# Ordering the heads' transposes and pooled products behind the second next projection product, with low output weights made by VectorE

## The chip, the core and the metric

The kernel runs on one core of a Trainium2 chip. The metric is the device time of one execution in microseconds (us); a kernel's time is the median of its runs.

## What is computed

One layer of a hybrid encoder, on two sequences (1024 and 2048 tokens of width 1024) that share their weights. `mem` is 256 further tokens for each sequence. Cut to what matters:

```python
h = rms_norm(x, norm_pre)
z = h @ w_in                                   # 1024 -> 2304 columns
u_pool, g_pool, q, k, v, g_attn, q_x, g_x = split(z)
pool_out = multiscale_pool(u_pool, pool_w, pool_scale) * silu(g_pool)   # windows 2, 4, 8, 16: (window mean - u) @ pool_w[g], scaled
q = rope(rms_norm(q per head, q_norm))         # 8 heads of 64
k = rope(rms_norm(k per head, k_norm))         # 2 heads of 64
attn_out = softmax(q k^T / 8) v * silu(g_attn)
k_m, v_m = split(rms_norm(mem, mem_norm) @ w_mem_kv)
x_out = softmax(q_x k_m^T / 8) v_m * silu(g_x)
y = x + rms_norm(concat(pool_out, attn_out, x_out) @ w_out, norm_post)
```

All inputs and outputs are float32.

## The kernel before

The program has two parts. In the first, up to about 700 us, the projections `h @ w_in` are made and their results stored to DRAM scratch; in the second, attention, output projection and final norm read them back. The second part's order is written out by hand and is not touched by the change.

**Stages of the projections.** The tokens are worked in super-blocks of 1024, each of two blocks of 512: first `mem`, then the short sequence ("prompt stage"), then the two halves of the long one ("first" and "second sample stage"). For each block the normalised input is transposed on TensorE (`pt` tiles, line 621) into `hT_hi` and `hT_lo`: each float32 number is kept as a rounded high part and the low rest, and a product is made of three matmuls (high with high, high with low, low with high). The columns of `w_in` are cut into six groups of 384, and a group is run over both blocks before the next. Their order is n1, ct0, n0, ct2, ct1, ct3. While a group runs, the next group's weights are loaded (`wraw`) and split, by ScalarE into `w_hi` (line 649) and by VectorE into `w_lo` (line 652).

- n1 and n0 make *natural* products (tokens on partitions, 384 columns): four tiles of 128 tokens per block. n1 holds two query heads, the two key heads and v; n0 the other six query heads.
- The ct groups make *transposed* products (128 columns on partitions, 512 tokens), three per block. ct0 holds the two pooling chunks (c = 0 and 1) and a gate.

Each product is 8 x 3 matmuls into one PSUM tile `pz` (four buffers), by `product` (lines 660 to 662).

**The heads' chain.** Behind each natural product, `norm_rope` turns the result into normalised, rotated heads: ScalarE copies it to `z` (723) and squares it to `sq` (724); VectorE sums per head (726) and scales (70); GpSimd raises to the power -0.5 (`rs`, 72) and multiplies by the rotary tables (`t1` 734, `sq` 739); VectorE adds and scales `t1` (745, 746; the profile's name for it is `t`). `heads_transposed` then transposes `t1` on TensorE into the PSUM tile `ptq` (758), ScalarE and VectorE split it into high and low (`qst`, 77 and 78), and SP's queue stores it. `z`, `sq`, `t1` and `qst` have two buffers each.

**The pooling chain.** Behind each pooling product, ScalarE copies it to `u` (842), GpSimd makes window sums by adding shifted copies (851, tiles `s2`, `s4`, `sm`, one buffer each), VectorE copies one half (864) and forms mean minus `u` in `sm` (872). TensorE multiplies by `pool_w` into `pm` (879), which shares its two PSUM buffers with `ptq`, and ScalarE scales the result into `s4` (881), from where it is stored.

**Output weights.** In the sample stages, sixteen pieces of `w_out` are split: a load into `woraw` (775), the high part by ScalarE (776), the low part `wost` by GpSimd (777), a store (778).

**What sets the order.** In the projections a scheduler orders each engine's instructions by a model of their durations; every engine then runs its own list strictly in order and waits on semaphores. `behind(e, first)` adds a dependence of instruction `e` on the last instruction in the list `first`. Buffers of a pool are handed out in program order.

Of the kernel before, what the change touches and what calls it, by code (L numbers as in the profile page):

```python
# [7 lines left out]
F32 = mybir.dt.float32  # L8
F32R = mybir.dt.float32r
AF = mybir.ActivationFunctionType  # L10
ALU = mybir.AluOpType
# [12 lines left out]
def encoder(ctx, tc, I, O):  # L24


    nc = tc.nc
# [8 lines left out]
    DQ = {}  # L36
# [9 lines left out]
    DP = [scratch(f"dp{s}", [128, 2, T]) for s, (_, T) in enumerate(SEQS)]  # L46
# [455 lines left out]
    for g in groups:  # L502
        n, c = first[g], g.chunks // 2
        g.early = g in pairs[0].groups
        at(n + (1.2 if g.kind == 1 and g.s == 0 else 0.2), g.load_late)
        k = 0
# [61 lines left out]
    with ExitStack() as p1:  # L568
# [70 lines left out]
        def weights(src, pieces):  # L639
# [13 lines left out]
                                               in1=hi[:, c, 0:n].bitcast(F32), op0=ALU.mult, op1=ALU.subtract)  # L653
            return hi, lo

        def product(ps, terms, beside=lambda: None):

            n = len(terms)
            for c, (sh, sl, mh, ml) in enumerate(terms):
                nc.tensor.matmul(ps, lhsT=sh, rhs=mh, start=c == 0, stop=False)  # L660
                nc.tensor.matmul(ps, lhsT=sh, rhs=ml, start=False, stop=False)  # L661
                nc.tensor.matmul(ps, lhsT=sl, rhs=mh, start=False, stop=c == n - 1)  # L662
                if c % 2:
                    beside()

        def natural(hT, w, i, col, width):

# [48 lines left out]
        def norm_rope(ps, parts, tt):  # L716

            n = sum(h for h, _ in parts)
            w = 64 * n
            z = ftwo.tile([128, 384], F32, name="z", tag="z")  # L720
            sq = ftwo.tile([128, 384], F32, name="sq", tag="sq")
            t1 = ftwo.tile([128, 384], F32, name="t1", tag="t1")
            nc.scalar.copy(out=z[:, 0:w], in_=ps[:, 0:w])
            nc.scalar.activation(out=sq[:, 0:w], in_=ps[:, 0:w], func=AF.Square)  # L724
            ss = ftwo.tile([128, 6], F32, name="ssh", tag="ssh")
            nc.vector.tensor_reduce(out=ss[:, 0:n],
                                    in_=sq[:, 0:w].rearrange("p (h d) -> p h d", d=64),
                                    axis=AX.X, op=ALU.add)
            r = rsqrt(ftwo, ss[:, 0:n], n, 64, f"rsh{n}")
            h0 = 0  # L730
            for heads, (C, S) in parts:
                cols = slice(64 * h0, 64 * (h0 + heads))
                v3 = "p (h d) -> p h d"
                nc.gpsimd.tensor_tensor(
                    out=t1[:, cols].rearrange(v3, d=64), in0=z[:, cols].rearrange(v3, d=64),
                    in1=C[:, tt:tt + 1].broadcast_to([128, heads, 64]), op=ALU.mult)
                v5 = "p (h x s r) -> p h x s r"
                for s in range(2):
                    nc.gpsimd.tensor_tensor(
                        out=sq[:, cols].rearrange(v5, x=2, s=2, r=16)[:, :, :, s],  # L740
                        in0=z[:, cols].rearrange(v5, x=2, s=2, r=16)[:, :, :, 1 - s],
                        in1=S[:, tt:tt + 1].rearrange("p n (x s r) -> p n x s r", x=2, s=2)[:, :, :, s]
                        .broadcast_to([128, heads, 2, 16]), op=ALU.mult)
                h0 += heads
            nc.vector.tensor_tensor(out=t1[:, 0:w], in0=t1[:, 0:w], in1=sq[:, 0:w], op=ALU.add)
            nc.vector.tensor_tensor(
                out=t1[:, 0:w].rearrange("p (h d) -> p h d", d=64),
                in0=t1[:, 0:w].rearrange("p (h d) -> p h d", d=64),
                in1=r.unsqueeze(2).broadcast_to([128, n, 64]), op=ALU.mult)
            return t1  # L750
# [3 lines left out]
        def heads_transposed(src, npair, keys=None):  # L754

            pt = pst.tile([128, 4, 128], F32, name="ptq", tag="ptq")
            for c in range(npair):
                nc.tensor.transpose(out=pt[:, c], in_=src[:, 128 * c:128 * c + 128], identity=ident)
            o = ftwo.tile([128, 2, 3, 128], F32R, name="qst", tag="qst")
            split(o[:, 0, 0:npair], o[:, 1, 0:npair], pt[:, 0:npair])  # L760
            if keys is not None:
                old = steps[keys % 2]
                d = pt[:, 1]
                if keys > 1:
                    d = ftwo.tile([128, 128], F32, name="kstep", tag="kstep")
                    nc.vector.tensor_tensor(out=d, in0=pt[:, 1], in1=old, op=ALU.subtract)
                split(o[:, 0, 2], o[:, 1, 2], d)
                nc.scalar.copy(out=old, in_=pt[:, 1])
            return o
        def split_w_out(n):  # L770

            c, x = n // 2, slice(512 * (n % 2), 512 * (n % 2) + 512)
            raw = ftwo.tile([128, 512], F32, name="woraw", tag="woraw")
            both = ftwo.tile([128, 2, 512], F32R, name="wost", tag="wost")
            behind(nc.sync.dma_start(out=raw, in_=I["w_out"][0, 128 * c:128 * c + 128, x]), gated)
            nc.scalar.copy(out=both[:, 0], in_=raw)
            nc.gpsimd.tensor_tensor(out=both[:, 1], in0=raw, in1=both[:, 0].bitcast(F32), op=ALU.subtract)
            nc.sync.dma_start(out=DWO[c][:, :, x].rearrange("x p f -> p x f"), in_=both.bitcast(F32))


        def store_heads(o, c, dst, j):
            nc.sync.dma_start(out=dst, in_=o[64 * j:64 * j + 64, :, c].bitcast(F32))

        def group_n0(s, b, hT, w):
            for i in range(4):
                tt = 4 * b + i
                ps = natural(hT, w, i, 0, 384)
                o = heads_transposed(norm_rope(ps, [(6, rope["q"])], tt), 3)
                for j in range(2):
                    nc.sync.dma_start(  # L790
                        out=DQ[s, tt // 2, 0][j, :, :, tt % 2],
                        in_=o[64 * j:64 * j + 64, :, 0:2].bitcast(F32))
                    store_heads(o, 2, DQ[s, tt // 2, 1][j, :, :, tt % 2, 0], j)

        def group_n1(s, b, hT, w):
            if not rope:
                rope_tables()
            rope_block(b)
            for i in range(4):
                tt = 4 * b + i  # L800
                ps = natural(hT, w, i, 0, 384)
                vst = ftwo.tile([128, 2, 64], F32, name="vst", tag="vst")
                nc.scalar.copy(out=vst, in_=ps[:, 256:384].rearrange("p (g d) -> p g d", d=64))
                nc.scalar.dma_start(out=DV[s][:, :, tt].rearrange("g p x -> p g x"), in_=vst)
                o = heads_transposed(norm_rope(ps, [(2, rope["q"]), (2, rope["k"])], tt), 2, tt)
                keys = slice(128 * tt, 128 * tt + 128)
                for j in range(2):
                    store_heads(o, 0, DQ[s, tt // 2, 1][j, :, :, tt % 2, 1], j)
                    store_heads(o, 2, DK[s][j][1:3, :, keys].rearrange("x d t -> d x t"), j)
                    nc.sync.dma_start(out=DK[s][j][0, :, keys], in_=o[64 * j:64 * j + 64, 0, 1].bitcast(F32))  # L810

        poolw = one.tile([128, 2, 128], F32, name="poolw")
        pscale = one.tile([128, 2], F32, name="pscale")
# [15 lines left out]
        def pool_chunk(s, b, c, ps):  # L829
# [15 lines left out]
                nc.vector.memset(u[:, 528:L], 0.0)  # L845
            s2 = one.tile([128, L], F32, name="s2", tag="s2")
            s4 = one.tile([128, L], F32, name="s4", tag="s4")
            sm = one.tile([128, L], F32, name="sm", tag="sm")

            def add(out, a, sh, lo, hi, rows_):  # L850
                nc.gpsimd.tensor_tensor(out=out[rows_, lo:hi], in0=a[rows_, lo - sh[0]:hi - sh[0]],
# [17 lines left out]
            if last:  # L869
# [2 lines left out]
            nc.vector.scalar_tensor_tensor(out=sm[:, lo:hi], in0=sm[:, lo:hi],  # L872
                                           scalar=invw[:, c:c + 1], in1=u[:, lo:hi],
                                           op0=ALU.mult, op1=ALU.subtract)
            at = lo
            while at < hi:
                n = min(512, hi - at)
                pm = pst.tile([128, 512], F32, name="pm", tag="ptq")
                nc.tensor.matmul(pm[:, 0:n], lhsT=poolw[:, c], rhs=sm[:, at:at + n],
                                 start=True, stop=True)  # L880
                nc.scalar.activation(out=s4[:, at:at + n], in_=pm[:, 0:n], func=AF.Copy, scale=pscale[:, c:c + 1])
                at += n
            t0 = 512 * b - 16
            nc.scalar.dma_start(out=DP[s][:, c, t0 + lo:t0 + hi], in_=s4[:, lo:hi])

        def gate_chunk(s, b, kind, c, ps):
            g = one.tile([128, 512], F32, name="gst", tag="gst", bufs=2)
# [78 lines left out]
        rope = {}  # L966
# [4 lines left out]
        for sb, (kind, s, nb, b0) in enumerate(SB):  # L971
            groups = groups_of(sb)
            nxt = []
            for gi, (src, pieces, run) in enumerate(groups):
# [5 lines left out]
                final = gi + 1 == len(groups)  # L980
                last = sb + 1 == len(SB)
                if last and gi == 3:
                    front.close()
                    front_open = False
                    early = ctx.enter_context(tc.tile_pool(name="early", bufs=1, side="right", reuse_waits="tile"))
                    open_early()
                    for g in loads.pop(-1):
                        g.load()
# [139 lines left out]
```

## Time and profile before

| | |
|---|---|
| median of 3 runs | 1708.17 us (1707.6 to 1708.54) |
| the profiled execution | 1707.39 us |
| its span, first to last instruction | 1705.6 us |
| TensorE busy | 1674.2 us of the span |
| VectorE, GpSimd, ScalarE busy | 1146.1, 844.2, 826.7 us |
| mean granted TensorE clock | 0.998 |

The profile shows one execution. In its rows PE is TensorE, PEld its weight loads, DVE VectorE, ACT ScalarE, POOL GpSimd and SP the queue that issues most DMAs. A row of a group of instructions gives the line, engine, operation, output<-inputs, the shapes and the count, then busy us and mean ns of one, then how long the engine stood idle just ahead of them and what ended that. A row in order of time begins with the start and the duration in us. A matmul's start is recorded, its end is modelled, and matmuls overlap, so distances from start to start are the safer measure.

### The profile page before, as it was taken

Reading aid. Unit: us, or ns where it says so; the run is one execution under the profiler, and the core shown is the slowest. Engines: PE = TensorE matmul, PEld = TensorE weight load, DVE = VectorE, ACT = ScalarE, POOL = GpSimd, SP = SyncE. Lnnn points to the kernel's source line nnn. Section 1 sums busy time; section 2 is a strip of 40 time slices with the busy share of each in tenths; the row PEclk is TensorE's granted clock in tenths of the full one; section 3 lists DMA queues with packets and bytes.
Section 4 is the critical chain, followed back from the end, with each engine's and each line's share of the span. In section 5 each row is a group of like instructions: output and inputs, shape, how many; then the busy total and the mean of one; then the engine's idle time right before and its main releaser. Section 6 shows DMA issues by size and latency. Waiting matters only on the chain. (4 is left out here: it accounts for less than half of the span.)

```text
span 1705.6 us, 26342 instructions
## 1 busy us (share of the span) xinstructions
PE 1674.2 (98%) x9400; PEld 1166.7 (68%) x9400; DVE 1146.1 (67%) x1791; ACT 826.7 (48%) x1392; POOL 844.2 (49%) x814
## 2 busy tenths in 40 slices
PE   7999999999999999999999999999999999999998
PEld 6988889798898987544555555655555555566566
DVE  6856316554164442698888888888888869877862
ACT  7543226423253330244566566666666655654541
POOL 1846105463054530167667676766666674331331
PEclk9999999999999999999999999999999999999999
DMA  7643636447564385462121211111121134323222
GB/s 238 192 130 103 170 100 183 142 130 194 172 188 122 97 215 134 124 205 105 57 69 51 76 62 50 65 61 57 63 75 63 57 108 140 106 91 102 70 93 93
DMA packets 161458, 194.07 MB, mean 114 GB/s; under 512 B 23584, under 2 KB 123056, under 8 KB 161328
## 3 DMA queue, kind: packets, MB, share of 16 engines
q1 hardware_dynamic: 127152, 174.56, 33.5%
q10 hardware_dynamic: 34176, 17.83, 3.5%
q8 instruction: 75, 1.23, 0.3%
q14 instruction: 55, 0.45, 0.1%
HBM read 128.61 MB, written 63.59 MB: 113 GB/s over the span
## 5 line engine op out<-in xcount | busy, mean ns | idle before, releaser
L247 POOL TENSOR_TENSOR z<-z,P 128x512 f32<-128x512 f32 x224 | 327.9, 1464 | 159.9 <-ACT P L233 152.5
L233 ACT ACTIVATE P<-S 128x1024 f32<-128x1024 f32 x344 | 334.5, 1024 | 111.9 <-PE S L231 68.2
L259 PE MATMUL acc<-P,V 128*64 128x512 f32 (+1 forms) x1472 | 318.9, 573 | 1.4 <-ACT P L233 0.5
L244 DVE TENSOR_TENSOR z<-z,P 128x512 f32<-128x512 f32 (+1 forms) x272 | 277.6, 1020 | 5.7 <-ACT P L233 5.5
L196 ACT COPY look<-N 128x512 f32<-128x512 f32 x258 | 152.2, 590 | 188.9 <-PE N L189 188.3
L660 PE MATMUL pz<-hT_hi,w_hi 128*128 128x512 f32 x592 | 234.1, 396 | 0.3 <-ACT sq L724 0.3
L661 PE MATMUL pz<-hT_lo,w_hi 128*128 128x512 f32 x592 | 232.5, 393 | 0.0
L662 PE MATMUL pz<-hT_hi,w_lo 128*128 128x512 f32 x592 | 231.5, 391 | 0.0
L259 PEld LDWEIGHTS acc<-P,V 128*64 128x64 f32 x1472 | 94.9, 136 | 174.5 <-issue 125.6
L197 DVE TENSOR_REDUCE nb<-N 128x1 f32<-128x512 f32 x258 | 176.6, 685 | 44.3 <-PE N L189 43.7
L199 DVE TENSOR_REDUCE nb<-look 128x1 f32<-128x512 f32 x258 | 175.9, 682 | 40.6 <-ACT look L196 39.3
L231 PE MATMUL S<-q,DH 64*128 64x512 f32 x1280 | 201.6, 392 | 0.0
L652 DVE SCALAR_TENSOR_TENSOR w_lo<-wraw,gaintok,w_hi 128x384 fp32r<-128x384 f32 x144 | 98.6, 742 | 90.1 <-ACT w_hi L649 90.1
L72 POOL TENSOR_TENSOR rs<-rs,mhalf 128x1 f32<-128x1 f32 (+2 forms) x76 | 75.0, 989 | 166.6 <-DVE rs L70 165.7
L189 PE MATMUL N<-KH,q 64*128 64x512 f32 x640 | 147.2, 455 | 3.0 <-ACT P L233 1.3
L660 PE MATMUL pz<-w_hi,hT_hi 128*128 128x384 f32 (+1 forms) x416 | 140.8, 338 | 3.2 <-ACT hT_hi L77 3.2
L662 PE MATMUL pz<-w_hi,hT_lo 128*128 128x384 f32 (+1 forms) x416 | 142.9, 344 | 0.0
L661 PE MATMUL pz<-w_lo,hT_hi 128*128 128x384 f32 (+1 forms) x416 | 140.8, 339 | 0.0
L396 PE MATMUL py<-wo_hi,mix 128*128 128x512 f32 x336 | 139.1, 414 | 0.0
L189 PEld LDWEIGHTS N<-KH,q 64*128 64x128 f32 x640 | 60.5, 183 | 114.5 <-issue 74.7
L231 PEld LDWEIGHTS S<-q,DH 64*128 64x128 f32 x1280 | 119.9, 185 | 23.7 <-issue 2.4
L397 PE MATMUL py<-wo_lo,mix 128*128 128x512 f32 x336 | 131.2, 391 | 0.0
(158 smaller groups left out, 2759.4 us busy)
## 6 DMA issues: line engine op xcount, KB each, us to landing
wraw<-w_in SPq DMA_DIRECT2D x15, 1536.0 KB
dg<-gst ACTq DMA_DIRECT2D x48, 256.0 KB
q<-dq SPq DMA_DIRECT2D x24, 512.0 KB
gz<-rows SPq DMA_DIRECT2D x72, 128.0 KB
x<-x_sample SPq DMA_DIRECT2D x16, 512.0 KB
dwo<-wost SPq DMA_DIRECT2D x16, 512.0 KB
xr<-x_sample SPq DMA_DIRECT2D x16, 512.0 KB
y_sample<-xr SPq DMA_DIRECT2D x32, 256.0 KB
```

What stands on the lines that cost most here:

```text
L189: nc.tensor.matmul(S[:, 512 * j:512 * j + 512], lhsT=self.q[h, 0, 128 * lane:128 * lane + 128], rhs=KH[self.kind][h, 512 * a:512 * a + 512 ...
L196: c = nc.scalar.copy(out=t[:, 0], in_=S[:, 1])
L197: m = nc.vector.tensor_reduce(out=out[:, 0:1], in_=S[:, 0:1], axis=AX.X, op=ALU.max, negate=True)
L199: nc.vector.tensor_reduce(out=out[:, 1:2], in_=t, axis=AX.X, op=ALU.max, negate=True)
L231: nc.tensor.matmul(S[:, at + x:at + x + w], lhsT=K, rhs=self.q[h, qx, x:x + w], start=False, stop=n == 2, skip_group_check=True)
L233: nc.scalar.activation(out=self.P[k].rearrange("p j q -> p (j q)"), in_=S, func=AF.Exp)
L244: e = nc.vector.tensor_tensor(out=z[:, cut:], in0=a[:, cut:], in1=P[:, cut:], op=ALU.add)
L247: nc.gpsimd.tensor_tensor(out=z[:, :cut], in0=a[:, :cut], in1=P[:, :cut], op=ALU.add)
L259: nc.tensor.matmul(self.acc[64 * j:64 * j + 64, x], lhsT=v, rhs=P[:, j, x], start=(k, i) == (0, 0), stop=k == self.chunks - 1, skip_group_ ...
L660: nc.tensor.matmul(ps, lhsT=sh, rhs=mh, start=c == 0, stop=False)
L661: nc.tensor.matmul(ps, lhsT=sh, rhs=ml, start=False, stop=False)
L662: nc.tensor.matmul(ps, lhsT=sl, rhs=mh, start=False, stop=c == n - 1)
```

## The change

- `later_by(n, f)` holds a piece of work back until n further products have been written down; `product` keeps its last matmul in `ended` and runs what is due.
- The heads' transposes with all that follows them (`finish_n0`, `finish_n1`) are held back by two products, and the first transpose depends on the last matmul of the product just written, so TensorE has it behind that product. `t1` has three buffers.
- The pooled product with its scaling and store (`pool_end`) is treated likewise. `sm` has two buffers, and the scaled result goes to a tile of its own, `po`, instead of `s4`.
- What is still held back in the last super-block is run ahead of its fourth group, before the pools of the projections' front are closed.
- The low part of the output weights is made by VectorE.

```diff
+        HEADS, POOLED = 2, 2
+        ended, waiting, products = [], [], []
+
+        def later_by(n, f):
+            waiting.append((len(products) + n, f))
+            waiting.sort(key=lambda x: x[0])
+
         def product(ps, terms, beside=lambda: None):
...
-                nc.tensor.matmul(ps, lhsT=sl, rhs=mh, start=False, stop=c == n - 1)
+                ended[:] = [nc.tensor.matmul(ps, lhsT=sl, rhs=mh, start=False, stop=c == n - 1)]
                 if c % 2:
                     beside()
+            products.append(ended[0])
+            while waiting and waiting[0][0] <= len(products):
+                waiting.pop(0)[1]()
...
-            t1 = ftwo.tile([128, 384], F32, name="t1", tag="t1")
+            t1 = ftwo.tile([128, 384], F32, name="t1", tag="t1", bufs=3)
...
-                nc.tensor.transpose(out=pt[:, c], in_=src[:, 128 * c:128 * c + 128], identity=ident)
+                (behind if c == 0 else lambda *_: None)(nc.tensor.transpose(out=pt[:, c], in_=src[:, 128 * c:128 * c + 128], identity=ident), ended)
...
-            nc.gpsimd.tensor_tensor(out=both[:, 1], in0=raw, in1=both[:, 0].bitcast(F32), op=ALU.subtract)
+            nc.vector.tensor_tensor(out=both[:, 1], in0=raw, in1=both[:, 0].bitcast(F32), op=ALU.subtract)
...
-                o = heads_transposed(norm_rope(ps, [(6, rope["q"])], tt), 3)
-                for j in range(2):
...
+                t = norm_rope(ps, [(6, rope["q"])], tt)
+                later_by(HEADS, lambda t=t, tt=tt: finish_n0(s, t, tt))
...
-            sm = one.tile([128, L], F32, name="sm", tag="sm")
+            sm = one.tile([128, L], F32, name="sm", tag="sm", bufs=2)
...
+            later_by(POOLED, lambda: pool_end(s, b, c, sm, lo, hi))
+
+        def pool_end(s, b, c, sm, lo, hi):
+            po = one.tile([128, 544], F32, name="po", tag="po")
             at = lo
             while at < hi:
...
-                nc.tensor.matmul(pm[:, 0:n], lhsT=poolw[:, c], rhs=sm[:, at:at + n],
-                                 start=True, stop=True)
-                nc.scalar.activation(out=s4[:, at:at + n], in_=pm[:, 0:n], func=AF.Copy, scale=pscale[:, c:c + 1])
+                behind(nc.tensor.matmul(pm[:, 0:n], lhsT=poolw[:, c], rhs=sm[:, at:at + n],
+                                        start=True, stop=True), ended)
+                nc.scalar.activation(out=po[:, at:at + n], in_=pm[:, 0:n], func=AF.Copy, scale=pscale[:, c:c + 1])
                 at += n
             t0 = 512 * b - 16
-            nc.scalar.dma_start(out=DP[s][:, c, t0 + lo:t0 + hi], in_=s4[:, lo:hi])
+            nc.scalar.dma_start(out=DP[s][:, c, t0 + lo:t0 + hi], in_=po[:, lo:hi])
...
                 if last and gi == 3:
+                    while waiting:
+                        waiting.pop(0)[1]()
```

How this moves instructions is shown at two places of the first sample stage, where group ct0's second block passes into group n0. The number behind a tile's name counts tiles and tells them apart. On TensorE before, the last pooled product (`pm_3429`) and the transposes of n0's first tile (`t1_3514`) stand together in a late product of n0:

```order
L661 MATMUL pz_3799<-w_lo_3220,hT_hi_2591 128x384
L662 MATMUL pz_3799<-w_hi_3219,hT_lo_2592 128x384
L660 MATMUL pz_3850<-w_hi_3219,hT_hi_2591 128x384
L879 MATMUL pm_3429<-sm_3422,poolw_155 128x512
L758 MATMUL ptq_3527<-ident_130,t1_3514 128x128 x3
L661 MATMUL pz_3850<-w_lo_3220,hT_hi_2591 128x384
```

On TensorE now, the same pooled product (`pm_3516`) stands in n0's second product:

```order
L669 MATMUL pz_3535<-w_hi_3189,hT_lo_2414 128x384
L667 MATMUL pz_3535<-w_hi_3189,hT_hi_2413 128x384
L668 MATMUL pz_3535<-w_lo_3190,hT_hi_2413 128x384
L901 MATMUL pm_3516<-sm_3424,poolw_155 128x512
L669 MATMUL pz_3535<-w_hi_3189,hT_lo_2414 128x384
```

and the transposes of n0's first tile (`t1_3522`) stand between its third product and its fourth:

```order
L668 MATMUL pz_3575<-w_lo_3190,hT_hi_2413 128x384
L669 MATMUL pz_3575<-w_hi_3189,hT_lo_2414 128x384
L768 MATMUL ptq_3600<-ident_130,t1_3522 128x128 x3
L667 MATMUL pz_3626<-w_hi_3189,hT_hi_2413 128x384
L668 MATMUL pz_3626<-w_lo_3190,hT_hi_2413 128x384
```

Both moved forward by several products, and apart from one another. On GpSimd before, the second pooling chunk's sums (`s2_3420`, `s4_3421`) have three tiles of heads and three weight steps between them:

```order
L851 TENSOR_TENSOR s2_3420<-u_3417 128x527
L777 TENSOR_TENSOR wost_3462<-woraw_3461,wost_3462 128x512
L734 TENSOR_TENSOR t1_3514<-z_3512,rope_707 128x384
L777 TENSOR_TENSOR wost_3692<-woraw_3691,wost_3692 128x512
L739 TENSOR_TENSOR sq_3513<-z_3512,rope_707 128x12x16 x2
L72 TENSOR_TENSOR rs_3519<-rs_3519,mhalf_124 128x6
L734 TENSOR_TENSOR t1_3565<-z_3563,rope_707 128x384
L739 TENSOR_TENSOR sq_3564<-z_3563,rope_707 128x12x16 x2
L72 TENSOR_TENSOR rs_3570<-rs_3570,mhalf_124 128x6
L777 TENSOR_TENSOR wost_3902<-woraw_3901,wost_3902 128x512
L739 TENSOR_TENSOR sq_3615<-z_3614,rope_707 128x12x16 x2
```

On GpSimd now:

```order
L869 TENSOR_TENSOR s2_3422<-u_3419 128x527
L869 TENSOR_TENSOR s4_3423<-s2_3422 128x525
L869 TENSOR_TENSOR sm_3424<-s4_3423 128x521
L869 TENSOR_TENSOR sm_3424<-s2_3422 64x512
L744 TENSOR_TENSOR t1_3522<-z_3520,rope_707 128x384
L749 TENSOR_TENSOR sq_3521<-z_3520,rope_707 128x12x16 x2
```

The four sums stand together ahead of the heads, and the weight steps have left this list. On VectorE, the third of them now stands within the chain of n0's third tile, ahead of its `rs` step:

```order
L736 TENSOR_REDUCE ssh_3616<-sq_3612 128x6
L787 TENSOR_TENSOR wost_3888<-woraw_3887,wost_3888 128x512
L70 TENSOR_SCALAR rs_3618<-ssh_3616 128x6
L78 TENSOR_TENSOR qst_3604<-ptq_3600,qst_3604 128x384
L755 TENSOR_TENSOR t1_3613<-t1_3613,sq_3612 128x384
```

Before, these VectorE steps followed one another with no weight step among them.

More of the change, by code (lines that the diff above doesn't have):

```diff
@@ L787, in group_n0, with finish_n0 @@
                 ps = natural(hT, w, i, 0, 384)
-                o = heads_transposed(norm_rope(ps, [(6, rope["q"])], tt), 3)
-                for j in range(2):
[L790 to L793, printed above, removed]
+                t = norm_rope(ps, [(6, rope["q"])], tt)
+                later_by(HEADS, lambda t=t, tt=tt: finish_n0(s, t, tt))
+        def finish_n0(s, t, tt):
+            o = heads_transposed(t, 3)
+            for j in range(2):
+                nc.sync.dma_start(
+                    out=DQ[s, tt // 2, 0][j, :, :, tt % 2],
+                    in_=o[64 * j:64 * j + 64, :, 0:2].bitcast(F32))
+                store_heads(o, 2, DQ[s, tt // 2, 1][j, :, :, tt % 2, 0], j)
         def group_n1(s, b, hT, w):
@@ L804, in group_n1, with finish_n1 @@
                 nc.scalar.dma_start(out=DV[s][:, :, tt].rearrange("g p x -> p g x"), in_=vst)
[L805 to L810, printed above, removed]
+                t = norm_rope(ps, [(2, rope["q"]), (2, rope["k"])], tt)
+                later_by(HEADS, lambda t=t, tt=tt: finish_n1(s, t, tt))
+        def finish_n1(s, t, tt):
+            o = heads_transposed(t, 2, tt)
+            keys = slice(128 * tt, 128 * tt + 128)
+            for j in range(2):
+                store_heads(o, 0, DQ[s, tt // 2, 1][j, :, :, tt % 2, 1], j)
+                store_heads(o, 2, DK[s][j][1:3, :, keys].rearrange("x d t -> d x t"), j)
+                nc.sync.dma_start(out=DK[s][j][0, :, keys], in_=o[64 * j:64 * j + 64, 0, 1].bitcast(F32))
         poolw = one.tile([128, 2, 128], F32, name="poolw")
```

## The prediction

> **What bounds the kernel now.** I read the page's busy times first, then the busy time by stage, then who TensorE waited for, and last its instructions in order of time around the longest waits. In the row of the stages the columns are the stretch, its length, busy time of TensorE, of its weight loads, VectorE, ScalarE and GpSimd with instruction counts, the granted clock, DMA share and GB/s.
>
> ```profile
> PE 1674.2 (98%) x9400; PEld 1166.7 (68%) x9400; DVE 1146.1 (67%) x1791; ACT 826.7 (48%) x1392; POOL 844.2 (49%) x814
> ...
> 300.00:400.00 100.00, 94.80 (x464) 82.39 (x463) 55.27 (x94) 37.11 (x82) 60.26 (x68) 0.98 0.49 151
> 400.00:700.00 300.00, 300.00 (x1448) 251.75 (x1447) 124.20 (x220) 94.97 (x208) 87.95 (x120) 1.00 0.54 150
> 700.00:1705.00 1005.00, 993.42 (x5984) 578.74 (x5982) 805.41 (x1153) 556.31 (x793) 570.76 (x428) 1.00 0.27 86
> ```
>
> TensorE is the bound throughout: every microsecond in which it waits in the projections (up to about 700 us) goes to the end, and nothing else can shorten the span. The change adds no TensorE work and takes none away, so its worth is the waits it removes less those it makes. Stretch 300 to 400 alone has 5.2 us without work. The waits of TensorE up to 760 us (total, times, longest), and the weight loads' idle time (last column) of the two kinds of instruction that the change moves:
>
> ```profile
> PE pm L879 <- DVE sm L872: 5.1, 3, 3.2
> PE ptq L758 <- DVE t L746: 1.8, 3, 0.8
> ...
> L758 PEld LDWEIGHTS ptq<-ident,t 128*128 128x128 f32 x120 | 15.2, 140 | 7.1 <-issue 1.3 <-PE ptq L758 1.2 <-PE pt L621 1.0
> L879 PEld LDWEIGHTS pm<-sm,poolw 128*128 128x128 f32 x32 | 5.6, 189 | 9.0 <-DVE sm L872 6.8 <-issue 1.7 <-POOL sq L739 0.2
> ```
>
> So the pooled products (pm) and the heads' transposes (ptq) cost at least 5.1 + 1.8 = 6.9 us, and at most the loads' 9.0 + 7.1 = 16.1 us, since that counts normal spacing too. The ends of matmuls are modelled, so I size each wait by start-to-start distance against the regular one. The two longest, in order of time:
>
> ```profile
> 336.34 0.35 PE L660 MATMUL pz<-w_hi,hT_hi 128*128 128x384 f32 x1
> 336.52 0.34 PE L661 MATMUL pz<-w_lo,hT_hi 128*128 128x384 f32 x1
> 340.06 1.14 PE L879 MATMUL pm<-sm,poolw 128*128 128x504 f32 x2 [3.20 <-DVE sm L872]
> ...
> 342.28 0.53 PE L660 MATMUL pz<-w_hi,hT_hi 128*128 128x384 f32 x1
> 342.60 0.53 PE L661 MATMUL pz<-w_lo,hT_hi 128*128 128x384 f32 x1
> ...
> 371.97 0.34 PE L660 MATMUL pz<-w_hi,hT_hi 128*128 128x384 f32 x1
> 373.75 1.12 PE L879 MATMUL pm<-sm,poolw 128*128 128x512 f32 x2 [1.44 <-DVE sm L872]
> ```
>
> Regular distance here is 0.17 to 0.18 (336.34 to 336.52). The wait to 340.06 costs 3.54 - 0.17 = 3.4 us; the one to 373.75 costs 1.78 - 0.17 = 1.6. After the first, matmuls start 0.32 apart (342.28 to 342.60) instead of 0.17: ten such distances, from 341 to 344.5, lose another 1.6 us to a lower clock (0.98 in that stretch's row). The 1.6 us wait is followed by no such rows. The same subtraction over all other places of pm and ptq gives 1.4 us more for pm and 3.7 for ptq. Sum: 3.4 + 1.6 + 1.4 + 3.7 + 1.6 = 11.7 us. I take this value; 6.9 and 16.1 + 1.6 = 17.7 are the bounds.
>
> By the Trainium skill, page "TensorE: Matmul & The Clock Gate", section "Part 1: The HAM clock gate", an idle window of about 3.4 us halves the array's rate and about 3.4 us of work restores it. By that rule the follow-on cost is half of 3.4, 1.7 us, and the trace agrees (1.6 after 3.5 us, none after 1.8); only waits above some 3 us would bring it again.
>
> **The change part by part.**
>
> *Heads' transposes behind the second next product (48 tiles), t1 with three buffers.* The same 120 transposes run, so no work is added. A natural product is 24 matmuls of 0.17, 4.2 us; with a tile's transposes (0.34 more) two of them give the chain about 9.0 us. What the chain needs, for the six heads of group n0 (POOL is GpSimd):
>
> ```profile
> L723 ACT COPY z<-pz 128x384 f32<-128x384 f32 x24 | 11.3, 477 | 31.2 <-PE pz L662 23.5 <-POOL sq L739 5.0 <-POOL t L734 2.7
> L734 POOL TENSOR_TENSOR t<-z,rope 128x384 f32<-128x384 f32 x24 | 27.1, 1143 | 30.4 <-PE ptq L758 22.2 <-ACT gst L888 4.2 <-ACT z L723 3.8
> L739 POOL TENSOR_TENSOR sq<-z,rope 128x192 f32<-128x192 f32 x48 | 31.7, 682 | 11.9 <-DVE ssh L726 11.8
> L72 POOL TENSOR_TENSOR rs<-rs,mhalf 128x6 f32<-128x6 f32 x24 | 33.3, 1391 | 0.2
> L746 DVE TENSOR_TENSOR t<-t,rs 128x384 f32<-128x384 f32 x24 | 15.5, 654 | 4.4 <-POOL rs L72 4.2
> ```
>
> 0.48 + 1.14 + 2 x 0.68 + 1.39 + 0.65 = 5.0 us, and about 0.7 for the handing over (estimate): 5.7, a slack of 3.3 us. GpSimd is busy 3.9 us of this per tile, under the product's 4.5, so no queue builds up. In the trace the n0 chains took longer because GpSimd stood 22.2 us waiting for transposes to free t1 (the L734 row). Three buffers end that: tile N then needs the transposes of tile N-3, which stand before product N is over.
>
> *Pooled products behind the second next product; two sm, own output tile po.* Chain for the second chunk of channels:
>
> ```profile
> L842 ACT COPY u<-pz 128x512 f32<-128x512 f32 x12 | 7.0, 583 | 4.8 <-PE pz L662 4.7
> L851 POOL TENSOR_TENSOR s<-u 128x527 f32<-128x527 f32 x4 | 4.8, 1203 | 6.5 <-ACT u L842 6.5
> L851 POOL TENSOR_TENSOR s<-s 128x525 f32<-128x525 f32 x4 | 4.2, 1062 | 9.9 <-DMA dp<-s 9.9
> L851 POOL TENSOR_TENSOR sm<-s 128x521 f32<-128x521 f32 x4 | 4.6, 1139 | 0.2
> L864 DVE COPY s<-sm 64x521 f32<-64x521 f32 x4 | 3.8, 942 | 20.4 <-POOL sm L851 20.4
> L851 POOL TENSOR_TENSOR sm<-s 64x512 f32<-64x512 f32 x4 | 4.9, 1225 | 1.1 <-DVE s L864 1.0
> L872 DVE SCALAR_TENSOR_TENSOR sm<-sm,invw,u 128x512 f32<-128x512 f32 x4 | 5.0, 1240 | 2.9 <-POOL sm L851 2.9
> ```
>
> These seven sum to 7.4 us, 8.5 with handing over and the edge columns. Two transposed products are 2 x 24 x 0.23 = 11 us. Slack 2.5. Before, this chain stopped 9.9 us for the output DMA that read s4 (row of the second add) and for sm, which the pooled product still held; both buffers are now free. The extra buffers issue nothing.
>
> *Low output weights from GpSimd to VectorE.* GpSimd gave 16 x 1.38 = 22.0 us; the nearest VectorE row of this size with two inputs in SBUF is 0.86, so VectorE gains 14 us in stages where it is about half idle (55 of 100 us at 300 to 400).
>
> ```profile
> L777 POOL TENSOR_TENSOR wost<-woraw,wost 128x512 fp32r<-128x512 f32 x16 | 22.0, 1380 | 70.4 <-ACT wost L776 50.9 <-DMA dg<-gst 17.5 <-DMA dq<-qst 2.0
> L244 DVE TENSOR_TENSOR z<-z,P 128x512 f32<-128x512 f32 x17 | 14.6, 857 | 0.0
> ...
> ACT wost L776 <- DMA woraw<-w_out: 24.9, 9, 6.2
> ```
>
> What queued behind it on GpSimd (rope, pow, pooled sums) is freed. In its place VectorE now stands still until ScalarE has the weights, which itself waited up to 6.2 us for the DMA. One of these stands in front of a tile's rs step in n0 of the first sample stage. Less the slack 3.3, that is 0 to 2.9 us once; I take 1.
>
> *What follows the transposes* (ScalarE cast, VectorE subtract and kstep, four to six stores per tile on SP's queue, the pooled output's DMA on ScalarE's) moves back by at most two products, 9 to 11 us. Loads of weights stand behind these stores, but a group's six to eight products last 33 us or more, and no wait of TensorE names w_hi or w_lo. Cost nothing while that holds; if a load came late by the whole 9 us, up to 9. In the last stage the lists are emptied ahead of the fourth group, so attention's loads are not later. Waits of TensorE on its own earlier matmuls are added at some 20 places: between 0 and the 0.16 by which a matmul's 0.34 exceeds its distance, up to 3 us; as the matmuls waited for are mostly old, I take 0.5. Another 0.5 goes to small waits at new places.
>
> Sum, against the profiled execution's own 1707.39 (span 1705.6): 1707.4 - 11.7 + 1 + 0.5 + 0.5 = 1697.7. The median of the runs is 0.8 above that execution, so 1698.5.
>
> **The rivals.**
>
> *Waits come back at the pinned places.* The pinned step cannot slide, so any chain over its slack stops TensorE. For it: the slack is only 2.5 to 3.3 us, and weight halves (w_lo) lie between the pooled steps on VectorE. Against: steady n1 tiles had room, z to finished t1 from 289.52 to 294.05:
>
> ```profile
> 289.52 0.39 ACT L723 COPY z<-pz 128x256 f32<-128x256 f32 x1
> 293.63 0.42 DVE L746 TENSOR_TENSOR t<-t,rs 128x256 f32<-128x256 f32 x1
> ...
> 165.84 0.48 ACT L723 COPY z<-pz 128x384 f32<-128x384 f32 x1 [2.09 <-POOL sq L739]
> 178.98 0.56 DVE L746 TENSOR_TENSOR t<-t,rs 128x384 f32<-128x384 f32 x1
> ```
>
> Of the six idle times half (3.5) and the clock's 1.6 come back: 1703.5, spread 1702 to 1706.
>
> *Slower.* The n0 chain really is as long as in the lower pair of rows, 13.7 us, whatever the buffers. Then the first tile of each of the three n0 groups stops TensorE 13.7 - 9.0 = 4.7 us and loses 1.6 to the clock: 3 x 6.3 = 18.9, against 11.7 saved: 1708.2 + 7 = 1715. It decides from a chain of 11.3 us (with the clock's loss) or 12.9 (without). Against it: that chain contains the t1 wait.
>
> *The move to VectorE gains nothing.* The copy from sm, 0.94 in the mean, took 1.40 beside a weight step on GpSimd:
>
> ```profile
> 335.24 1.40 DVE L864 COPY s<-sm 64x521 f32<-64x521 f32 x1
> ```
>
> If the two engines exclude each other, the three weight steps by n0's first tiles each hold GpSimd 0.86 and wait for one of its steps, about 1.27: 3 x 2.13 = 6.4, less 3.3 of slack, is 3.1 us: about 1701.5. The Trainium skill's page "SBUF — State Buffer", section "Who interferes with whom", says this of a VectorE tensor_tensor with both inputs in SBUF against GpSimd's reads; it speaks against the move, the stretched copy fits it, and no run here isolates it.
>
> *No effect:* the scheduler had hidden more than I count, and the waits only change places: 1705 to 1709.
>
> **How the numbers follow.** Forecast 1695 to 1702: 0.61, likeliest 1698.5. More gained, as the looser GpSimd queue also shortens other waits (bound 17.7 saved): 0.06. Waits come back: 0.16. Exclusion: 0.05. No effect: 0.06. Slower: 0.06. About 0.2%, 3.4 us, is what a measurement of this kernel can tell from no change. Faster than 1704.8: 0.61 + 0.06 + 0.05 + 0.12 of the come-back case = 0.84; same: the other 0.04 and 0.05 of no effect = 0.09; slower: 0.07. The range 1694 to 1705 leaves out 0.04 below and 0.16 above.
>
> **What would show it.** Right: TensorE's waits for sm and t together under 2 us; no stretch of 0.32 distances and clock 1.00 at 300 to 400; GpSimd no longer waiting for ptq or for the dp DMA; the weight step on VectorE at 0.7 to 1.0; 700 to the end unchanged in length. Wrong: ptq waits of several microseconds at the first tiles of n0, waits on w_lo, or half-clock rows at new places.

## The result, and the profile after

| | before | after |
|---|---|---|
| median, same chip, 5 runs each | 1708.17 us (1706.57 to 1709.9) | 1697.83 us (1697.33 to 1698.69) |
| profiled execution | 1707.39 us | 1697.95 us |
| its span | 1705.6 us | 1695.8 us |

After takes 0.994 of the time before, 95% interval 0.9925 to 0.9954: 10.3 us less. The prediction was 1698.5 us, range 1694 to 1705.

TensorE is still the bound, as the page's busy times say:

```profile
PE 1668.9 (98%) x9400; PEld 1164.5 (69%) x9400; DVE 1148.1 (68%) x1807; ACT 826.7 (49%) x1392; POOL 818.2 (48%) x798
```

The stages, from the rows of busy time by stretch (length, then TensorE, its weight loads, VectorE, ScalarE and GpSimd, the granted clock, DMA share, GB/s); the last stretch is drawn 10 us earlier than before:

```profile
100.00:200.00 100.00, 100.00 (x494) 87.34 (x493) 47.38 (x77) 34.90 (x70) 40.59 (x46) 1.00 0.47 134
300.00:400.00 100.00, 99.17 (x489) 86.17 (x488) 57.94 (x98) 36.95 (x81) 50.09 (x56) 1.00 0.55 160
400.00:690.00 290.00, 290.00 (x1406) 243.72 (x1405) 121.64 (x225) 92.73 (x203) 73.81 (x110) 1.00 0.52 147
690.00:1695.00 1005.00, 992.86 (x5984) 578.52 (x5983) 806.12 (x1153) 557.56 (x793) 570.56 (x428) 1.00 0.27 86
```

Stretch 300 to 400 went from 94.80 to 99.17 us of work and from clock 0.98 to 1.00. Stretch 100 to 200, in the prompt stage, was not shown before; its row of before had

```profile
100.00:200.00 100.00, 97.80 (x482) 84.16 (x481) 48.38 (x79) 35.83 (x72) 46.40 (x49) 1.00 0.46 136
```

Counting the 3024 projection matmuls off one by one in both traces says where the time came back: the kernel after is 4.0 us ahead by 185 us, 10.2 us ahead by 405 us, and no further behind that: the last projection matmul starts at 704.8 before and at 695.0 after, and from it to the end the two take 1000.7 and 1000.8 us. So all of it comes from two places, where group ct0 passes into n0 in the prompt stage and in the first sample stage; the second sample stage gave nothing.

Of the two kinds of waits that the prediction listed, one row is left among TensorE's waits up to 760 us:

```profile
PE pm L901 <- DVE sm L890: 0.8, 1, 0.8
```

and the weight loads of the two kinds of instruction, up to 700 us, stood idle (last column) for:

```profile
L768 PEld LDWEIGHTS ptq<-ident,t 128*128 128x128 f32 x120 | 15.8, 140 | 2.9 <-issue 0.2
L901 PEld LDWEIGHTS pm<-sm,poolw 128*128 128x128 f32 x32 | 5.9, 189 | 3.8 <-issue 1.9 <-ACT po L903 1.2
```

The waits for `t` are gone from the list and the waits for `sm` fell from 5.1 us to 0.8; the loads' idle time fell from 7.1 and 9.0 to 2.9 and 3.8. By start-to-start distance less the regular one, summed over every place, pm went from 6.5 to 1.1 us and ptq from 3.2 to 0.2 (the prediction had 6.4 and 3.7 for the kernel before). The table below uses this measure.

### The profile page after: what moved, and what is told of

It reads as the page before. It is cut to its first block, busy times and chain, and to the rows that moved or that the text cites. A ratio compares the mean times of both kernels' runs of the same rounds, so it can differ in the third digit from the quotient of the medians.

```text
span 1695.8 us, 26424 instructions
## 1 busy us (share of the span) xinstructions
PE 1668.9 (98%) x9400; PEld 1164.5 (69%) x9400; DVE 1148.1 (68%) x1807; ACT 826.7 (49%) x1392; POOL 818.2 (48%) x798
## 5 line engine op out<-in xcount | busy, mean ns | idle before, releaser
L72 POOL TENSOR_TENSOR rs<-rs,mhalf 128x1 f32<-128x1 f32 (+2 forms) x76 | 74.7, 984 | 244.6 <-DVE rs L70 244.6
L652 DVE SCALAR_TENSOR_TENSOR w_lo<-wraw,gaintok,w_hi 128x384 fp32r<-128x384 f32 x144 | 88.4, 668 | 80.9 <-ACT w_hi L649 80.8
```

## The experiments

Every kernel below was timed against the kernel before on the same chip. The columns: the two sums just described, in the profiled execution; and the time from GpSimd's first add to its second in the pooled chain of the second chunk (`s<-u` to `s<-s`), in the first block of the prompt stage and in that of the first sample stage. The kernel before took 1707.7 us beside e1 to e4, 1706.6 beside e5 to e8 and 1707.1 beside e9 to e12, so gains are taken from each run's own partner and not between rows. The profiled executions of e2 and e11 were 2.0 and 1.3 us longer than their medians.

| kernel | median us | ratio to before, 95% | pm, ptq us | first to second add, us |
|---|---|---|---|---|
| before | 1708.17 | | 6.5, 3.2 | 19.0, 15.4 |
| after | 1697.83 | 0.9940 (0.9925-0.9954) | 1.1, 0.2 | 1.3, 1.3 |
| e1 heads' part | 1697.23 | 0.9939 (0.9927-0.9951) | 0, 0.5 | 11.8, 11.1 |
| e2 pooled part | 1698.54 | 0.9952 (0.9937-0.9967) | 0.4, 4.1 | 1.5, 1.3 |
| e3 VectorE part | 1702.29 | 0.9970 (0.9958-0.9982) | 1.8, 2.9 | 19.1, 12.4 |
| e4 all but VectorE | 1697.92 | 0.9945 (0.9932-0.9957) | 0, 0.2 | 1.3, 1.7 |
| e5 buffers alone | 1698.48 | 0.9951 (0.9938-0.9965) | 0, 2.0 | 1.6, 1.3 |
| e6 order, old t1 and sm | 1697.56 | 0.9945 (0.9933-0.9958) | 0.9, 1.5 | 2.1, 1.3 |
| e7 one product | 1697.75 | 0.9948 (0.9934-0.9962) | 0, 1.6 | 1.6, 1.5 |
| e8 pooled three | 1695.29 | 0.9935 (0.9922-0.9947) | 0, 0.2 | 1.3, 1.3 |
| e9 three | 1698.48 | 0.9948 (0.9935-0.9962) | 0, 0 | 1.3, 1.3 |
| e10 own output | 1701.95 | 0.9970 (0.9959-0.9981) | 0, 5.2 | 1.5, 1.3 |
| e11 third t1 | 1707.31 | 1.0004 (0.9995-1.0014) | 6.8, 2.1 | 17.1, 15.2 |
| e12 heads' order | 1698.02 | 0.9950 (0.9938-0.9963) | 0, 1.6 | 10.5, 11.4 |

### One part at a time

The theory at this point was the prediction's: each part removes its own waits, so the parts add up.

**e1, the heads' part alone** (with the third `t1`). Against the kernel after:

```diff
-            later_by(POOLED, lambda: pool_end(s, b, c, sm, lo, hi))
+            pool_end(s, b, c, sm, lo, hi, s4)      # output into s4, one sm, no behind
...
-            nc.vector.tensor_tensor(out=both[:, 1], ...)
+            nc.gpsimd.tensor_tensor(out=both[:, 1], ...)
```

> Only the heads' part of the change (transposes behind the second next product, t1 with three buffers). Theory (the gain is TensorE's removed waits, each part its own): the ptq waits, 3.7 us, go, the pm waits and the low clock stay: about 1704.5, 1703 to 1706. Rival A (the move of the weight step from GpSimd brings the gain): no change, 1707 to 1709. Rival B (the buffers bring it, not the order): not told apart here.

Measured 1697.23 us: the whole gain, though nothing of the pooled part is there. A miss.

**e2, the pooled part alone** (heads as before, two `t1`, weights on GpSimd).

```diff
-            later_by(HEADS, lambda t=t, tt=tt: finish_n0(s, t, tt))
+            finish_n0(s, t, tt)                    # and finish_n1; no behind
```

> Only the pooled part (pm behind the second next product, two sm, own output tile). Theory: the pm waits, 6.4 us, and the half clock, 1.6 us, go: about 1700, 1698.5 to 1702; ptq waits remain at n0's tiles. Rival A: no change, 1707 to 1709.

Measured 1698.54 us, at the lower edge of the range. The waits for `t` stay, as expected (ptq 4.1).

**e3, the low weights on VectorE alone.** The kernel before with one line:

```diff
-            nc.gpsimd.tensor_tensor(out=both[:, 1], in0=raw, in1=both[:, 0].bitcast(F32), op=ALU.subtract)
+            nc.vector.tensor_tensor(out=both[:, 1], in0=raw, in1=both[:, 0].bitcast(F32), op=ALU.subtract)
```

> Only the low output weights moved to VectorE. Theory: GpSimd is not what the waits hang on, so within 1.5 us of the kernel before: 1706.5 to 1709.5. Rival A: most of the 10 us, 1698 to 1701.

Measured 1702.29 us, 5 us faster where the theory had next to nothing.

**e4, the whole change but with the weights on GpSimd** (the same line, reversed).

> The whole change except that the low output weights stay on GpSimd. Theory: nearly the changed kernel, 1697.5 to 1700; the first sample stage's n0 chains may come 1.3 us later per weight step and use up slack. Rival A: 1706 or more.

Measured 1697.92 us, against 1697.83 for the whole: as expected.

Alone, the three gain 10.4, 9.1 and 5.4 us; together they gain 10.3. They don't add: each takes away much the same waits. The theory of separate waits fell, and the question became what those waits hang on.

### Buffers or order

**e5, the buffers alone**: three `t1`, two `sm`, own `po`; nothing is held back, weights on GpSimd.

```diff
+            t1 = ftwo.tile([128, 384], F32, name="t1", tag="t1", bufs=3)
+            sm = one.tile([128, L], F32, name="sm", tag="sm", bufs=2)
+            po = one.tile([128, 544], F32, name="po", tag="po")
```

> Only the buffers: a third t1, a second sm and an own output tile po, each pooled product and transpose where the scheduler puts it, weights on GpSimd. Revised theory (TensorE loses time only where a chain comes later than the place that the scheduler gave its product; the chip's chain shortens with the buffers, and the place moves only as far as the scheduler's own reckoning of the same buffers moves it): the 9.9 us wait for the output DMA that read s4 goes, so the 3.4 us wait and its 1.6 of half clock at 340 go; the small ptq and pm waits stay: 1700 to 1703. Rival (buffers are all that counts, order nothing): 1697.5 to 1698.5. Other rival (order is all): 1706.5 to 1709.

Measured 1698.48 us: the rival's value, and the theory's 1700 to 1703 missed. With free buffers the scheduler itself puts the products where the chains allow it.

**e6, the change with the old buffers** (`po` stays).

```diff
-name="t1", tag="t1", bufs=3
+name="t1", tag="t1", bufs=2
-name="sm", tag="sm", bufs=2
+name="sm", tag="sm"
```

> The changed kernel with two t1 and one sm as before (po stays). With the products pinned two behind, tile N's rope step needs the transposes of tile N-2, which stand behind product N: with two buffers GpSimd waits for them, and n0 chains grow by up to the time from z to those transposes' end. Theory: PE stops at n0's first tiles or a few places, 1 to 6 us: 1699 to 1704. Rival (buffers don't matter once the order is pinned): 1697.5 to 1698.5.

Measured 1697.56 us: with the order given, the two extra buffers don't matter. The theory's 1699 to 1704 missed.

**e7, one product instead of two.**

```diff
-        HEADS, POOLED = 2, 2
+        HEADS, POOLED = 1, 1
```

> HEADS, POOLED = 1, 1: each step behind the next product instead of the second next. Theory that place against chain length decides: n0 chains of 6.3 to 8.6 us against one product of 4.2 to 4.5 stop TensorE about 2 to 2.5 us at every second n0 tile (24 tiles: about 12 x 2.3 = 28 us), the second pooled chunk 8.5 to 10.6 against 5.5 in four places about 4 us each with 1.6 of half clock where over 3 us: 16 to 22 us; n1 little: 1735 to 1750. Rival (TensorE's place is not what matters, since GpSimd and buffers were the cause): 1697.5 to 1703.

Measured 1697.75 us: far off the theory's 1735 to 1750. The trace says why. The dependence on the next product only forbids an earlier place; it doesn't set the place. In the prompt stage the first n0 tile's `z` starts at 126.24 and its transposes at 134.70, 1.75 products later, although one would be allowed; the scheduler reckons with the chain and goes further back by itself.

**e8, the pooled product one later.**

```diff
-        HEADS, POOLED = 2, 2
+        HEADS, POOLED = 2, 3
```

> HEADS, POOLED = 2, 3: the pooled product one product later. Theory: the one wait left for sm in the changed kernel (1.0 us of excess at 323.14) goes, nothing else changes: 1696.5 to 1697.3. Rival (two sm buffers no longer do, since the pooled product of chunk 0 then stands behind the first products of the next kind, and GpSimd waits for sm): 1697.8 to 1700.

Measured 1695.29 us (1695.2 to 1697.49): the pm wait left in the kernel after (1.1 us) is gone, as the theory had it. The size is beyond it: of the 2.6 us between the two profiled spans, 1.3 lie behind the last projection matmul (999.5 against 1000.8 us), where nothing was edited. It is the fastest version run, but its interval overlaps that of the kernel after.

### Which of the edits

Left were: one buffer, or the heads' order without any.

**e10, own output alone**: the kernel before, with `po` instead of `s4` for the pooled product's output.

```diff
+            po = one.tile([128, 544], F32, name="po", tag="po")
-                nc.scalar.activation(out=s4[:, at:at + n], in_=pm[:, 0:n], ...)
+                nc.scalar.activation(out=po[:, at:at + n], in_=pm[:, 0:n], ...)
```

> The kernel before with one edit: the pooled product's output goes to a tile of its own (po) instead of s4. Theory (the second add of the pooled chain waited for the output DMA that read s4, 9.9 us in all, and that chain is the one that stopped TensorE at 340 and 373): chains of the second chunk fall from 24 to 40 us to under 12, the two long waits and the half clock go, small waits stay: 1699 to 1702. Rival (sm and t1 hold the chain as long): 1704.5 to 1709.

**e11, a third `t1` alone.**

```diff
+            t1 = ftwo.tile([128, 384], F32, name="t1", tag="t1", bufs=3)
```

> The kernel before with one edit: three t1 instead of two. GpSimd's 22.2 us of waiting for transposes shrink; the pooled chain still waits for the output DMA. Theory: n0 chains shorter, the ptq waits (3.2 us by distances) mostly go, pooled waits of 5 to 6.5 us stay unless the order moves: 1703 to 1706. Rival (any edit that makes the scheduler place the work anew loses the few waits, since they are accidents of one order): 1697 to 1699.

**e12, the heads' order alone**, two `t1` as before.

```diff
+                later_by(HEADS, lambda t=t, tt=tt: finish_n0(s, t, tt))   # and n1, with behind
```

> The kernel before with only the heads' transposes put behind the second next product, with two t1 as before: the heads' part without its buffer. Theory (buffers shorten the chains, order alone doesn't): GpSimd waits for the transposes still, pooled waits stay: 1703 to 1708. Rival (a new placement is enough): 1697 to 1699.

**e9, everything one product later**, four `t1`.

```diff
-        HEADS, POOLED = 2, 2
+        HEADS, POOLED = 3, 3
```

> The changed kernel with HEADS, POOLED = 3, 3 and four t1: every step one product later than in the changed kernel. Theory (more slack, nothing waits): no pm and no ptq wait, 1695.2 to 1697.3, as with 2, 3. Rival (stores and keys come too late for what follows, or GpSimd waits for sm): 1698 to 1702.

e11 measured 1707.31 us (no change, 1.0004), outside both ranges; e10 1701.95, inside the theory's; e12 1698.02, the rival's value; e9 1698.48, the rival's value. So "any new placement does it" fell with e11, though there GpSimd's order around the longest wait stayed what it was, and "order alone does nothing" fell with e12. e9 has no pm or ptq wait and still gives nothing over two products: a wait for the block's own transposes at 63 us grew (2.9 us from start to start, 2.0 in the kernel after), and the granted clock was low there (third figure from the right, 0.57; the columns are those of the stages above):

```profile
62.00:66.00 4.00, 2.94 (x12) 2.84 (x13) 3.96 (x11) 0.86 (x2) 2.58 (x7) 0.57 0.61 169
```

The rest I can't place.

**What the waits hang on.** The trace of before around its longest wait of TensorE (340.06), GpSimd in order of time:

```profile
315.97 1.06 POOL L851 TENSOR_TENSOR s<-u 128x527 f32<-128x527 f32 x1 [3.49 <-ACT u L842]
330.82 0.55 POOL L72 TENSOR_TENSOR rs<-rs,mhalf 128x1 f32<-128x1 f32 x1 [13.78 <-DVE rs L70]
331.34 1.06 POOL L851 TENSOR_TENSOR s<-s 128x525 f32<-128x525 f32 x1
333.09 0.55 POOL L72 TENSOR_TENSOR rs<-rs,mhalf 128x1 f32<-128x1 f32 x1 [0.69 <-DVE u L840]
333.61 1.06 POOL L851 TENSOR_TENSOR sm<-s 128x521 f32<-128x521 f32 x1
334.62 1.73 POOL L777 TENSOR_TENSOR wost<-woraw,wost 128x512 fp32r<-128x512 f32 x1
```

Between the first and the second add stands a step of the *next block's input norm* (L72, one column), and GpSimd waits 13.78 us for it. Behind that step are VectorE's `rs`, ScalarE's `junk` (the squares of the norm) and the load of `x`. ScalarE's row, then SP's queue:

```profile
329.40 1.06 ACT L614 ACTIVATE junk<-x 128x1024 bf16<-128x1024 f32 x1 [8.97 <-DMA x<-x_sample]
...
317.86 1.24 SPq L782 DMA_DIRECT2D dk<-qst  x2
319.15 0.60 SPq L810 DMA_DIRECT2D dk<-qst  x1
319.79 0.59 SPq L635 DMA_DIRECT2D wraw<-w_in  x1
320.48 2.59 SPq L602 DMA_DIRECT2D x<-x_sample  x2
```

The load of `x` stands in SP's queue behind the stores of n1's transposed heads, some 0.6 us of queue each, and the queue also stood 3.2 us waiting for such a store's data. So two chains that share no data meet twice, in SP's queue and in GpSimd's list: heads' stores, then `x`, then the norm, then the pooled add, then TensorE. e12, which only moves the heads' transposes and stores back, has the loads of `x` ahead of most of those stores, and between the adds a weight step and nothing of the norm:

```profile
303.34 1.00 SPq L602 DMA_DIRECT2D x<-x_sample  x2
...
310.90 1.20 POOL L869 TENSOR_TENSOR s<-u 128x527 f32<-128x527 f32 x1
321.04 1.29 POOL L787 TENSOR_TENSOR wost<-woraw,wost 128x512 fp32r<-128x512 f32 x1 [8.94 <-ACT wost L786]
322.29 1.12 POOL L869 TENSOR_TENSOR s<-s 128x525 f32<-128x525 f32 x1
```

Its chain is still long (18.6 us from `u` to `sm`, 24.7 before), but its product stands 1.8 us behind the chain's end, and TensorE doesn't wait. What counts is thus the chain's end against the product's place, not the chain's length. e10 comes to it from the other side: with the own output tile the second add stands directly behind the first, ahead of the norm, and the pm waits are gone (6.5 to 0). e11 has the x loads at 320.36 as before, the norm between the adds as before, and the waits as before:

```profile
330.50 0.56 POOL L72 TENSOR_TENSOR rs<-rs,mhalf 128x1 f32<-128x1 f32 x1 [13.58 <-DVE rs L70]
```

and, from its list of TensorE's waits,

```profile
PE pm L901 <- DVE sm L890: 5.4, 4, 2.8
```

All the runs agree on this. The first of the two loads of `x` that these norm steps need goes out at 320.5 in the kernel before and at 320.4 in e11, and between 285.9 and 305.6 in the twelve others; and those two alone have a wait of 3.2 or 2.8 us at this product, the others 0.8 at most. (The profiled execution of e11 differs from that of the kernel before in two more things: it lost nothing to the clock, and 2.7 us to a product that waited for ScalarE's `gst` at 656.65.)

e3 shows the second thing at this place. The norm isn't between its adds, and the second add waits for the store that reads `s4`:

```profile
329.35 1.06 POOL L869 TENSOR_TENSOR s<-s 128x525 f32<-128x525 f32 x1 [11.19 <-DMA dp<-s]
```

In the kernel before it was not the store: by its semaphore the one issued at 319.45 had landed at 323.2, more than 7 us ahead of the norm step. What e3 has shorter is the rest: without the weight step among the adds, from the second add to the end of `sm` it takes 6.3 us, against 8.7 before. Its loads of `x` go out at 302.16 and 306.63.

The second long wait (373.75, 1.6 us) is another case. Between the adds of its chain stand heads and weight steps, 22.9 us in all, and no norm step; in e12 it is 15.1 us, and the product, 11.0 us earlier than before, again stands 2.2 us behind its chain. Why the scheduler puts it there wasn't followed, nor were the small waits of the prompt stage (4.0 us of the gain). That these waits go too in most of the runs is in the table's sums; their cause stays open.

**Why e10 gains only half.** Its pm waits are gone, as its theory had it, but ptq grew from 3.2 to 5.2 us and the low clock is back at another place, so that it met its range is in part luck. TensorE stops for long once, in n0 of the first sample stage, with a weight step on GpSimd ahead of the heads' steps:

```profile
355.92 1.29 POOL L787 TENSOR_TENSOR wost<-woraw,wost 128x512 fp32r<-128x512 f32 x1 [5.35 <-ACT qst L77]
357.17 1.17 POOL L749 TENSOR_TENSOR sq<-z,rope 128x192 f32<-128x192 f32 x2
...
354.88 0.62 ACT L786 CAST wost<-woraw 128x512 fp32r<-128x512 f32 x1 [6.10 <-DMA woraw<-w_out]
...
362.95 0.67 PE L768 MATMUL ptq<-ident,t 128*128 128x128 f32 x3 [3.54 <-DVE t L756]
```

The step waits for ScalarE's cast (its row names ScalarE's instruction behind that), which waits 6.10 us for the load of the weights; the rope steps of a tile that is ready stand behind it. e2, also with the weights on GpSimd, has the like (a 2.9 us wait for `t` at 363.07). The third part of the change takes this step off GpSimd; no run adds it to e10 or e2, so that it would cure this wait is argued, not shown. In e4 and e5 it wasn't needed: there the weights are on GpSimd too, and the ptq sums are 0.2 and 2.0.

**What is still lost after.** The one wait left, at 323.14, comes along a third path, ScalarE and VectorE:

```profile
318.99 0.37 ACT L77 CAST qst<-ptq 128x256 fp32r<-128x256 f32 x1 [5.96 <-DMA dq<-qst]
319.40 0.43 DVE L78 TENSOR_TENSOR qst<-ptq,qst 128x256 fp32r<-128x256 f32 x1 [5.09 <-ACT qst L77]
320.05 0.43 DVE L882 COPY s<-sm 64x521 f32<-64x521 f32 x1
...
323.14 1.08 PE L901 MATMUL pm<-sm,poolw 128*128 128x504 f32 x2 [0.83 <-DVE sm L890]
```

With the heads' finish moved back, `qst` (two buffers) is asked for again before its store has landed; ScalarE waits 5.96 us, VectorE 5.09 behind it, and the pooled copy L882 is late by 3.5 us. (Up to 700 us ScalarE waited longer for such stores before, 21.5 us against 10.9, but not once between 300 and 345.) e8 moves the product behind that.

## Why the prediction was right, and where it was not

**The sum.** It held: 11.7 us of waits less 2 gave 9.7, measured 9.8 in span. Its terms, against the same measure after: pm 6.5 to 1.1, ptq 3.2 to 0.2, half clock 1.6 to 0, together 10.0 of 11.3 (ptq was over-read by half a us). Against it stands 1.2 more in the block's own transposes (pt, 1.8 to 3.0); that leaves 8.8, and the last 1.0 I can't place. So the 2 us that were allowed for new waits fit 1.3 left in pm and ptq and 1.2 new in pt in size, but not in place, which is luck. The two long waits and the clock, 6.6 us, lie in the first sample stage, where the traces part by 6.2 between 185 and 405 us.

**The step that failed: which wait stopped the pooled chain.** The prediction said that "this chain stopped 9.9 us for the output DMA that read s4". The row is right, but it is a sum over a whole run. GpSimd's waits of the kernel before between 500 and 600 us alone hold all of it (total, times, longest):

```profile
POOL s L851 <- DMA dp<-s: 10.1, 2, 9.9
```

There every pooled product stood 1.4 us or more behind its chain, and TensorE lost nothing. At 316 to 331 GpSimd's wait was the 13.78 us for the next block's norm, and the store there had long landed. The sum needs only that TensorE's waits go, whatever caused them, and the change cures both; so the time came out right with the cause in the wrong place, which is in part luck.

**Each part its own waits.** The prediction's sum counts the waits once, rightly, but goes through the change part by part, and the expectations of e1 and e3 took each part to remove its own waits. Wrong: the whole gain is a ceiling of about 10 us that several edits reach alone. VectorE's part, which the prediction gave a cost of 1 us and no gain of its own, is worth 5.4 us alone, and in the whole (0.9940 with it, 0.9945 without) less than the intervals can tell.

**"The pinned step cannot slide."** Wrong: e7. It can slide later, by the scheduler's own reckoning; the rival built on it, waits that come back at pinned places, has its basis only where that reckoning falls short of the chip's chain.

**Chains and prices.**

```profile
L787 DVE TENSOR_TENSOR wost<-woraw,wost 128x512 fp32r<-128x512 f32 x16 | 11.5, 722 | 49.9 <-ACT wost L786 49.9
L744 POOL TENSOR_TENSOR t<-z,rope 128x384 f32<-128x384 f32 x24 | 24.9, 1039 | 19.7 <-ACT z L733 19.7
L749 POOL TENSOR_TENSOR sq<-z,rope 128x192 f32<-128x192 f32 x48 | 29.0, 625 | 16.4 <-DVE ssh L736 16.2
L756 DVE TENSOR_TENSOR t<-t,rs 128x384 f32<-128x384 f32 x24 | 24.7, 1028 | 15.1 <-POOL rs L72 15.1
L882 DVE COPY s<-sm 64x521 f32<-64x521 f32 x4 | 1.7, 430 | 3.2 <-POOL sm L869 3.2
```

The weight step took 0.72 us on VectorE (0.86 taken). n0's chains took 6.3 to 8.7 us in the first sample stage and 4.6 in the steady part of the second, against 5.7; their slack there was 0.7 to 2.7 and about 4.1, against 3.3. GpSimd's rope steps no longer wait for ptq (22.2 us before; the L744 row names only `z` now), and its adds no longer for dp. VectorE's standstill, costed at 1, is there, in the chain of n0's third tile in the first sample stage:

```profile
353.64 0.69 DVE L787 TENSOR_TENSOR wost<-woraw,wost 128x512 fp32r<-128x512 f32 x1 [1.58 <-ACT wost L786]
```

That chain took 8.0 us, against 6.5 for the tile ahead of it, and still had 0.7 us of slack, so TensorE lost nothing.

**What follows the transposes at no cost.** Nearly right: no weights came late, but the stores moved back hold `qst` and make the wait at 323.14 above, 1.0 us by start-to-start distance.

**Exclusion.** The rival named the weight step; it is elsewhere. L756 grew from 654 to 1028 ns in the mean, and L882 fell from 942 to 430. Neither decided anything, since n0's slack takes the 0.4 us.

## What to carry to other kernels

When TensorE waits for a chain, read who stands *between* that chain's own steps in each in-order list, and follow that stranger back: here an unrelated norm step, held by a load that stood behind unrelated stores, made the longest wait. A sum of waits in a list of a whole run must be looked up by window before it explains a certain stall. And where several edits loosen the same chain, don't add their gains: count the waits once, as a ceiling, and test one edit at a time.

## What was not expected of the hardware

**VectorE beside GpSimd.** The same operation of VectorE on 128x384, 4 us apart in e10: the first began while GpSimd worked on L744 (346.82, 1.02 us), the second while GpSimd was idle.

```profile
346.89 1.36 DVE L756 TENSOR_TENSOR t<-t,rs 128x384 f32<-128x384 f32 x1 [0.28 <-POOL rs L72]
350.60 0.56 DVE L756 TENSOR_TENSOR t<-t,rs 128x384 f32<-128x384 f32 x1 [0.27 <-POOL rs L72]
...
346.82 1.02 POOL L744 TENSOR_TENSOR t<-z,rope 128x384 f32<-128x384 f32 x1
```

A factor of 2.4, on a step that the prediction had not thought of. The Trainium skill's page "SBUF — State Buffer", section "Who interferes with whom", names a VectorE tensor_tensor with both inputs in SBUF as one that contends with GpSimd's reads; these rows agree with it. No run here takes the two apart with all else equal.

**The clock after a short wait.** In e11 the pooled product at 339.77 came after a 2.83 us wait, and the matmuls behind it start a regular 0.17 apart. In e2 a 2.90 us wait was followed by 1.7 us of regular distances and then by seven of 0.32, and so was one of 3.20 in the kernel before (ten of them, 1.3 us later); after 3.54 us in e10 nine of 0.32 came almost at once. In e2, where it begins:

```profile
364.32 0.34 PE L669 MATMUL pz<-w_hi,hT_lo 128*128 128x384 f32 x1
364.49 0.47 PE L667 MATMUL pz<-w_hi,hT_hi 128*128 128x384 f32 x1
364.75 0.53 PE L668 MATMUL pz<-w_lo,hT_hi 128*128 128x384 f32 x1
365.07 0.53 PE L669 MATMUL pz<-w_hi,hT_lo 128*128 128x384 f32 x1
```

In e9 the low clock of 62 to 66 us came with a wait of only 2.54 us among the block's own transposes. So the length of a wait alone doesn't decide, and the loss can set in with a delay; the prediction's "only waits above some 3 us" doesn't hold. The Trainium skill's page "TensorE: Matmul & The Clock Gate", section "Part 1: The HAM clock gate", says that the window of about 3.4 us runs freely and lowers the clock when it was idle. The delay fits that; that the window has to be idle as a whole doesn't fit e2 and e9, where from one start to the next only 3.24 and 2.88 us passed.

**Issuing stores takes long.** A store of transposed heads holds SP's queue for about 0.6 us (the L810 row). With four to six for each tile, the loads of `x` went out at 320.48 in the kernel before, behind them, and at 303.34 in e12. Not all of the 17 us is issuing: from 313.31 on the queue issued nearly without a break, just before that it had waited 3.2 us for a store's data.
